# W block sums w21+w22 and (w21+w22)-w11 of the up projection: issued on POOL instead of DVE

## The chip, the core and the metric

One core of a Trainium2 chip runs the whole program. The metric is the device time of one execution in microseconds (us). Engines in the profile: PE is the matrix engine (PEld its weight loads), DVE the vector engine, ACT the scalar engine, POOL the GpSimd engine, SP the queue that issues most DMAs.

## The reference

A trunk of two layers works on 1024 tokens of width 1024. Each layer is an attention mixer followed by a squared-ReLU MLP, with norms, shifts, scales and gates around both. The change touches the first half of the MLP only:

```python
def squared_relu_mlp(h, w_up, w_down):      # w_up: 1024 x 4096, w_down: 4096 x 1024
    a = jax.nn.relu(h @ w_up)
    return (a * a) @ w_down
```

## The kernel before

**Seven products in place of eight.** `h @ w_up` is done for two hidden tiles of 128 at a time, called a pair, `q` = 0 to 15. Tokens (two halves of 512), input width (two halves of 512) and the two hidden tiles give a 2x2x2 block product, which is computed by Winograd's scheme with seven half-size products, named 1, 2, 6, 5, 7, 3, 4 in their order. They need four sums of weight blocks per pair. w11, w21 (first half of the width, first and second hidden tile) come with one DMA, w12, w22 with another. Sum 1 is w21+w22 (line 1322), sum 2 is sum 1 - w11 (line 1323), sum 3 is w11-w21 (line 1329), sum 4 is w12 - sum 2 (line 1333). Product 6 takes sum 2, product 5 sum 1, product 7 sum 3, product 3 sum 4. Each sum is a tile `ws` of 128x512 f32.

**Preparation of a product.** `prep(i)` (line 1306) forms the sum if the product needs one, then ACT rounds it to the high part (line 1339, tile `wt`), DVE subtracts that from the sum to get the low part (line 1340), and PE runs 12 matmuls for the product (`mm3`, lines 572 to 574: high x high, high x low, low x high, four times). The low part is the stationary operand of line 574. `before(i)` issues `prep` for a product `AHEAD` = 3 products ahead of its use, and the load of a pair some two products before that.

**What follows a product.** `evac` (line 1370 on DVE, from the matmul's bank; 1372, 1382 and 1383 on ACT) adds, applies ReLU and squares, into tiles `u`. After product 4 of a pair, `combine` forms five sums of the squared halves on POOL (line 1415 four times, tiles `sx`; line 1426 once, tile `sy`), which SP writes to DRAM (lines 1419 to 1427) for the down projection.

**Stretches.** Products 1 and 2 of the first six pairs (`PAIRS0`) run first, so a pair of the first six has only five products left when its sums are needed; the other ten pairs have seven. Beside them runs a side load (`ada`, lines 311 to 323): DMA loads `adaw` and DVE multiplies and adds.

**Order.** The order in the code is a list of steps that spreads preparations, products and side work; the framework then arranges the instructions of each engine by its own estimates of their times, so that POOL's order in the trace is not that of the code. At run time every engine and every queue takes its instructions in order. Tiles come from shared rings: 40 slots (`wt`, `u`, `sx`, the second half of the weights), 3 `raw` tiles (`adaw` and the first half of the weights), 8 `t2` tiles (`ws`, `sy`). A new tile waits for the last reader of the one that it replaces.

Of the kernel before, what the change touches and what calls it, by code (L numbers as in the profile page):

```python
# [93 lines left out]
class Trunk:  # L94
# [1126 lines left out]
    def up_setup(self, w_up, col):  # L1221
# [6 lines left out]
        nc = self.nc  # L1228
# [77 lines left out]
        def prep(i):  # L1306

            q, p = order[i]
            w = wraw[q]
            early = i < at[0]  # L1310
            t = nc.vector.tensor_tensor

            def new(n):
                sums[n] = four(self.t2("ws"))
                return sums[n]

            if p == 1:
                r = w[11]
            elif p == 2:
                r = w[12]  # L1320
            elif p == 6:
                t(new(1), w[21], w[22], op=ALU.add)
                t(new(2), sums[1], w[11], op=ALU.subtract)
                r = sums[2]
            elif p == 5:
                r = sums.pop(1)
            elif p == 7:
                r = new(3)
                nc.gpsimd.tensor_tensor(r, w.pop(11), w.pop(21), op=ALU.subtract)
                sums.pop(3)  # L1330
            elif p == 3:
                r = new(4)
                nc.gpsimd.tensor_tensor(r, w.pop(12), sums.pop(2), op=ALU.subtract)
                sums.pop(4)
            else:
                r = w.pop(22)
            s = self.slot("wt", F32R, [P, 2, 512])
            hi, lo = (four(s[:, y]) for y in range(2))
            nc.scalar.activation(hi, r, AF.Copy)  # L1339
            nc.vector.tensor_tensor(lo, r, hi.bitcast(F32), op=ALU.subtract)  # L1340
            left[i] = s
            if early and p == 2 or p == 4:
                wraw.pop(q)
# [5 lines left out]
        def before(i):  # L1349

            out = [lambda n=n: prep(n) for n in range(len(order)) if when(n) == i]
            if i in (0, 1, 2):
                out += [lambda q=q: load(q, True) for q in (3 + i,) if q < PAIRS0]
            for q in range(n_q):
                if i == (2 if q == 0 else when(at[q] - 2)):
                    out.append(lambda q=q: load(q, False))
            return out
# [479 lines left out]
```

## Time and profile before

| | us |
|---|---|
| median of three runs | 2547.33 |
| lowest, highest | 2542.2, 2547.57 |
| the profiled execution | 2548.21 |
| its span, first to last instruction | 2546.4 |
| PE busy | 2399.9 (94%) |
| DVE busy | 1924.9 (76%) |
| ACT busy | 1403.2 (55%) |
| POOL busy | 1325.5 (52%) |

The table's busy times are sums over the span. Matmuls are pipelined and their ends are modelled, so that the idle time in front of a PE instruction says more than PE's busy share. A wait names the instruction that released it.

### The profile page before, as it was taken

The numbers are of one execution on the slowest core, as the hardware profiler recorded it, in microseconds if no ns is written. First come the engines' busy times: TensorE is split into PE (matmuls) and PEld (weight loads), VectorE is DVE, ScalarE is ACT, GpSimd is POOL, SyncE is SP. The second block draws the span as 40 slices with busy tenths as digits, with TensorE's granted clock in tenths as the row PEclk, the third lists the DMA queues.
The fourth block names the chain that finished last, engine by engine and source line by source line (L and its number), as shares of the span: only waits on it lengthen the run. The fifth ranks groups of instructions, "written<-read, shape, count | busy, mean of one in ns | idle before, by whom it ended". The sixth has DMA issues, their size and how long they took to land.

```text
span 2546.4 us, 36695 instructions
## 1 busy us (share of the span) xinstructions
PE 2399.9 (94%) x11974; PEld 1991.6 (78%) x11974; DVE 1924.9 (76%) x3723; ACT 1403.2 (55%) x2959; POOL 1325.5 (52%) x1308
## 2 busy tenths in 40 slices
PE   6989999999998988999999999978999899999997
PEld 4779788888887766777778887867877688888886
DVE  7866479999895477877899768667767766787756
ACT  4632268888983463444435445367876355545433
POOL 4320566564672146555764722577744654594533
PEclk8999999999999999999999999998999999999999
DMA  7367723131226635556888754444323545597654
GB/s 279 100 224 229 237 88 96 39 92 42 84 71 149 141 116 189 201 191 201 321 324 324 236 189 163 138 128 125 75 76 128 186 168 183 192 318 240 230 183 173
DMA packets 239288, 437.15 MB, mean 172 GB/s; under 512 B 19236, under 2 KB 122872, under 8 KB 239096
## 3 DMA queue, kind: packets, MB, share of 16 engines
q1 hardware_dynamic: 210296, 405.44, 47.3%
q0 software_dynamic: 28800, 29.36, 4.8%
q8 instruction: 94, 1.54, 0.2%
q14 instruction: 98, 0.80, 0.1%
HBM read 320.42 MB, written 114.31 MB: 171 GB/s over the span
## 4 chain that ended last, share of the span: by engine, by line
PE 40%; DVE 6%; POOL 3%; issue 2%; DMA 2%; ACT 2%; SPq 0%; POOLq 0%; DVEq 0%; ACTq 0%
PE b L574 13%; PE b L572 13%; PE b L573 12%; POOL sx L1415 1%; DVE ada L323 1%; PE b L880 1%; DMA w<-in_mlp_w_up_dram 1%; DVE hl L1251 1%; PE o L925 1%; DVE p L884 1%; PE b L903 1%; DVE wt L1340 1%; DMA adaw<-in_ada_w_dram 0%; POOL qv L637 0%; POOL wr L1473 0%
## 5 line engine op out<-in xcount | busy, mean ns | idle before, releaser
L572 PE MATMUL b<-hh,wt 128*128 128x512 f32 x896 | 355.0, 396 | 17.0 <-ACT wt L1339 16.9
L574 PE MATMUL b<-hh,wt 128*128 128x512 f32 x896 | 350.9, 395 | 11.9 <-DVE wt L1340 11.6
L573 PE MATMUL b<-st,st 128*128 128x512 f32 x896 | 350.3, 391 | 4.9 <-DVE st L1489 4.9
L573 PE MATMUL b<-hl,wt 128*128 128x512 f32 x896 | 352.1, 393 | 0.0
L574 PE MATMUL b<-st,st 128*128 128x512 f32 x896 | 349.0, 390 | 0.0
L572 PE MATMUL b<-st,st 128*128 128x512 f32 x896 | 330.7, 390 | 1.6 <-DVE u L1370 1.6
L888 ACT ACTIVATE p<-p,nm 128x256 f32<-128x256 f32 (+7 forms) x384 | 250.7, 657 | 56.5 <-DVE nm L884 55.3
L1028 POOL TENSOR_SCALAR p<-p,rl,nsam 128x640 f32<-128x640 f32 (+7 forms) x256 | 199.5, 791 | 139.5 <-DVE rl L1026 93.1
L910 DVE TENSOR_TENSOR pT<-b,pT 128x512 fp32r<-128x512 f32 (+1 forms) x334 | 215.0, 657 | 19.5 <-ACT pT L909 19.1
L1488 ACT ACTIVATE st<-wr 128x1024 fp32r<-128x1024 f32 (+1 forms) x128 | 122.6, 958 | 193.2 <-POOL wr L1474 87.4
L1489 DVE TENSOR_TENSOR st<-wr,st 128x1024 fp32r<-128x1024 f32 (+1 forms) x128 | 188.3, 1471 | 53.6 <-ACT st L1488 30.1
L1489 DVE TENSOR_TENSOR st<-sr,st 128x1024 fp32r<-128x1024 f32 (+1 forms) x128 | 200.4, 1566 | 33.0 <-ACT st L1488 30.8
L572 PEld LDWEIGHTS b<-hh,wt 128*128 128x128 f32 x896 | 170.1, 190 | 59.3 <-ACT wt L1339 25.4
L574 PEld LDWEIGHTS b<-hh,wt 128*128 128x128 f32 x896 | 169.9, 190 | 55.7 <-DVE wt L1340 20.5
L909 ACT ACTIVATE pT<-b 128x512 fp32r<-128x512 f32 (+1 forms) x334 | 186.3, 579 | 43.2 <-PE b L903 41.8
L573 PEld LDWEIGHTS b<-st,st 128*128 128x128 f32 x896 | 168.5, 188 | 42.4 <-DVE st L1489 7.8
L903 PE MATMUL b<-ident,p 128*128 128x128 f32 x1296 | 193.5, 273 | 5.7 <-DVE nm L884 4.1
L1340 DVE TENSOR_TENSOR wt<-ws,wt 128x512 fp32r<-128x512 f32 x128 | 139.5, 1101 | 77.4 <-ACT wt L1339 76.8
L572 PEld LDWEIGHTS b<-st,st 128*128 128x128 f32 x896 | 168.6, 188 | 37.2 <-DVE u L1370 2.4
L573 PEld LDWEIGHTS b<-hl,wt 128*128 128x128 f32 x896 | 170.1, 190 | 34.6
L574 PEld LDWEIGHTS b<-st,st 128*128 128x128 f32 x896 | 168.6, 188 | 34.9
L925 PE MATMUL o<-pT,kv 128*128 128x512 f32 x484 | 193.1, 437 | 1.8 <-DVE pT L910 1.4
(277 smaller groups left out, 6060.3 us busy)
## 6 DMA issues: line engine op xcount, KB each, us to landing
adaw<-in_ada_w_dram SPq DMA_DIRECT2D x96, 512.0 KB, 4.9
sr<-s SPq DMA_DIRECT2D x96, 512.0 KB, 4.7
wr<-in_mlp_w_down_dram SPq DMA_DIRECT2D x96, 512.0 KB, 5.9
w<-in_mlp_w_up_dram SPq DMA_DIRECT2D x76, 512.0 KB, 4.8
s<-sx SPq DMA_DIRECT2D x64, 512.0 KB, 4.0
x<-x SPq DMA_DIRECT2D x48, 512.0 KB, 3.8
s<-u SPq DMA_DIRECT2D x64, 256.0 KB, 2.3
we<-in_mlp_w_down_dram SPq DMA_DIRECT2D x64, 256.0 KB, 3.9
```

The lines of the kernel that those rows point to most:

```text
L572: mm(out, s[0], m[0], start=first, stop=False)
L573: mm(out, s[0], m[1], start=False, stop=False)
L574: mm(out, s[1], m[0], start=False, stop=last)
L888: self.nc.scalar.activation(p, p, AF.Exp, scale=-1.0, bias=nm, accum_out=l)
L903: nc.tensor.transpose(pt[:, g * P:(g + 1) * P], p[:, cols], self.ident)
L909: nc.scalar.activation(x[:, 0, 0:w], pt[:, 0:w], AF.Copy)
L910: nc.vector.tensor_tensor(x[:, 1, 0:w], pt[:, 0:w], x[:, 0, 0:w].bitcast(F32), op=ALU.subtract)
L925: nc.tensor.matmul(out, s, m[:, z], start=n == 0 and z == 0, stop=n == len(tiles) - 1 and z == 1)
L1028: nc.gpsimd.tensor_scalar(ps[g], ps[g], rl[:, g:g + 1], gate[:, g, b:b + 1], op0=ALU.mult, op1=ALU.mult)
L1340: nc.vector.tensor_tensor(lo, r, hi.bitcast(F32), op=ALU.subtract)
L1488: nc.scalar.activation(hi, r, AF.Copy)
L1489: nc.vector.tensor_tensor(lo, r, hi.bitcast(F32), op=ALU.subtract)
```

## The change

The function that `prep` calls for sums 1 and 2 becomes POOL's. Sums 3 and 4 are already on POOL, the low parts (line 1340) stay on DVE. Nothing else is edited.

```diff
             early = i < at[0]
-            t = nc.vector.tensor_tensor
+            t = nc.gpsimd.tensor_tensor
...
                 t(new(1), w[21], w[22], op=ALU.add)
                 t(new(2), sums[1], w[11], op=ALU.subtract)
```

Only the two calls of lines 1322 and 1323 use `t`.

## Rows read from the trace of the kernel before

**Rows 1.** The page's busy times of all engines over the span.
```profile
PE 2399.9 (94%) x11974; PEld 1991.6 (78%) x11974; DVE 1924.9 (76%) x3723; ACT 1403.2 (55%) x2959; POOL 1325.5 (52%) x1308
```
**Rows 2.** Busy time by stretch; columns: stretch, length, then busy us (instructions) of each engine.
```profile
925.00:1045.00 120.00, 107.40 (x458) 84.14 (x457) 97.07 (x111) 59.06 (x97) 63.19 (x39) 1.00 0.51 170
1045.00:1225.00 180.00, 175.26 (x780) 142.31 (x779) 134.99 (x177) 85.79 (x146) 94.76 (x64) 0.99 0.57 196
1925.00:2045.00 120.00, 108.95 (x451) 84.89 (x450) 90.70 (x105) 54.52 (x90) 61.52 (x42) 0.97 0.42 145
2045.00:2225.00 180.00, 180.00 (x802) 148.69 (x801) 124.37 (x164) 93.02 (x152) 97.42 (x70) 1.00 0.52 182
```
**Rows 3.** PE's waits, 925:1045, then 1925:2045: total us, times, longest us.
```profile
PE b L574 <- DVE wt L1340: 6.9, 6, 2.9
PE b L572 <- ACT wt L1339: 5.6, 4, 2.5
...
PE b L572 <- ACT wt L1339: 9.0, 7, 2.6
PE b L574 <- DVE wt L1340: 1.9, 3, 0.9
```
**Rows 4.** PE's wait for a high part in 1045:1225, same view.
```profile
PE b L572 <- ACT wt L1339: 0.3, 1, 0.3
```
**Rows 5.** Instructions by line, whole span: count, then ns min/median/max.
```profile
L1322 DVE TENSOR_TENSOR ws<-w,w x32: 673/692/1785, 929.9 to 2196.7; 128x512 f32<-128x512 f32 x32
...
L1329 POOL TENSOR_TENSOR ws<-w x32: 1295/1314/2312, 923.1 to 2211.4; 128x512 f32<-128x512 f32 x32
...
L1415 POOL TENSOR_TENSOR sx<-u,u x64: 1282/1734/2264, 962.4 to 2241.0; 128x512 f32<-128x512 f32 x64
```
**Rows 6.** DVE's groups in 925:1045: busy us, mean ns, idle before, releaser.
```profile
L1322 DVE TENSOR_TENSOR ws<-w,w 128x512 f32<-128x512 f32 x7 | 5.9, 841 | 9.0 <-DMA w<-in_mlp_w_up_dram 9.0
L1323 DVE TENSOR_TENSOR ws<-ws,w 128x512 f32<-128x512 f32 x7 | 5.3, 755 | 0.0
```
**Rows 7.** POOL's waits in 925:1045: total us, times, longest us.
```profile
POOL ws L1333 <- DVE ws L1323: 37.2, 6, 12.5
```
**Rows 8.** Timeline of one pass, by engine: start, us, instruction, [idle before, releaser].
```profile
972.62 0.69 DVE L1322 TENSOR_TENSOR ws<-w,w 128x512 f32<-128x512 f32 x1 [2.48 <-DMA w<-in_mlp_w_up_dram]
...
973.83 0.68 DVE L1323 TENSOR_TENSOR ws<-ws,w 128x512 f32<-128x512 f32 x1
...
974.65 1.27 POOL L1333 TENSOR_TENSOR ws<-w,ws 128x512 f32<-128x512 f32 x1 [5.48 <-DVE ws L1323]
...
975.29 0.50 PE L572 MATMUL b<-hh,wt 128*128 128x512 f32 x1 [2.49 <-ACT wt L1339]
```
**Rows 9.** Timeline of a pass of the second layer, DVE and PE.
```profile
2003.75 0.69 DVE L1322 TENSOR_TENSOR ws<-w,w 128x512 f32<-128x512 f32 x1 [1.88 <-DMA w<-in_mlp_w_up_dram]
...
2005.89 0.50 PE L572 MATMUL b<-hh,wt 128*128 128x512 f32 x1 [2.60 <-ACT wt L1339]
```
**Rows 10.** Timeline, DVE's longest wait for weights and PE's next wait.
```profile
952.55 0.69 DVE L1322 TENSOR_TENSOR ws<-w,w 128x512 f32<-128x512 f32 x1 [5.14 <-DMA w<-in_mlp_w_up_dram]
...
955.93 0.50 PE L574 MATMUL b<-hh,wt 128*128 128x512 f32 x1 [0.91 <-DVE wt L1340]
```
**Rows 11.** Two lines of DVE, whole span: ns min/median/max.
```profile
L1370 DVE TENSOR_TENSOR u<-b,u x224: 645/679/693, 923.6 to 2230.0; 128x512 f32<-128x512 f32 x112
...
L1340 DVE TENSOR_TENSOR wt<-ws,wt x128: 672/1106/1779, 943.1 to 2214.7; 128x512 fp32r<-128x512 f32 x128
```
**Rows 12.** Timeline of a later pass, DVE and POOL.
```profile
1074.80 0.69 DVE L1322 TENSOR_TENSOR ws<-w,w 128x512 f32<-128x512 f32 x1 [0.20 <-DMA w<-in_mlp_w_up_dram]
...
1081.22 1.29 POOL L1415 TENSOR_TENSOR sx<-u,u 128x512 f32<-128x512 f32 x1 [8.38 <-ACT u L1383]
```
**Rows 13.** Timeline of SP's queue, two neighbouring issues.
```profile
981.05 0.32 SPq L1421 DMA_DIRECT2D s<-sx  x1
982.74 0.38 SPq L547 DMA_DIRECT2D w<-in_mlp_w_up_dram  x1
```

## The prediction

> **What bounds the kernel now.** I read the page's busy times first: PE is busy for 94% of the span and no other engine for more than 76% [rows 1]. So a change on DVE or POOL counts only where PE stands still. Next come the stretches in which the up projection runs, two per layer [rows 2]. The first of each layer (925 to 1045 us and 1925 to 2045 us, the six pairs with five products left) leaves PE idle for 12.6 and 11.1 us of 120; the second leaves 4.7 us of 180 and nothing. A matmul takes 180/802 = 0.224 us in the stretch without a gap, so a product of 12 takes 2.7 us. The reader should see that all that this change can win or lose at small scale lies in some 24 us of idle time at the start of the two up projections, and that the other pairs, 18 or so of the 32 passes, stand behind a full PE.
>
> Then I read what ends PE's waits there [rows 3]. PE waits 14.6 us for high parts from ACT and 8.8 us for low parts from DVE. The largest are waits for the high part of product 6, and the timeline shows the chain that ends in one: the weights land, DVE forms sum 1 at 972.62, does one evacuation in between, forms sum 2 from 973.83 to 974.51, ACT rounds it, and PE starts at 975.29 after 2.49 us of idling [rows 8]. In the second layer the same chain starts at 2003.75 and ends in an idle time of 2.60 us [rows 9]. Seven of PE's waits for high parts follow a sum 2 in this way, four in the first layer and three in the second. In these passes POOL is idle too: it waits for sum 2 with sum 4 next in its queue, 5.48 us in the pass shown [rows 8] and 37.2 us in six passes of the first layer [rows 7]. After sum 4 come the five sums of `combine`, and SP's next load of weights stands behind the write of such a sum [rows 13]. So the early passes form a loop: load, sums 1 and 2, sum 4, five `combine` sums, next load. What makes sum 2 later makes the whole loop later, and PE with it.
>
> **The change, part by part.** It removes 64 sums from DVE, 32 per line, and adds 64 to POOL. No DMA, no semaphore value by hand and no tile is added.
>
> *Cost of a sum.* On DVE the median is 0.692 us, and the same shape on POOL takes 1.314 us at the median, 1.295 at the least and 2.312 at the most [rows 5].
>
> *The path in the early passes.* DVE's pair takes 0.841 + 0.755 = 1.60 us there by means [rows 6], and mostly an evacuation of 0.68 us stands between the two [rows 8, 11], which costs some 0.6 us: 2.2 us from the first start to the second end. POOL's pair has nothing in between: 2 x 1.314 = 2.6 us undisturbed. The lower bound of the change of path is thus +0.4 us, and with two evacuations in between, as at some passes, -0.2. The upper bound is a pair in which both POOL instructions are disturbed as the median `combine` sum is, 2 x 1.734 = 3.5 us [rows 5], so +1.3. I take +0.6 us, nearer the undisturbed end, since DVE has evacuations to do at that moment, which read a bank and show no disturbance (645 to 693 ns over 224 of them [rows 11]). Seven passes: 7 x 0.6 = **+4.2 us**, between -1.4 and +9.1.
>
> *What leaves DVE.* In the early passes DVE stands still for 9.0 us before sum 1, waiting for weights [rows 6], with evacuations and low parts queued behind it. That wait moves to POOL, where sum 4 and the `combine` sums are queued behind it; but POOL waits at this place today, for sum 2 [rows 7], so it costs nothing new. For DVE it is a gain where PE waited for a low part that stood behind it: at 952.55 DVE has waited 5.14 us and PE stands for 0.91 us at 955.93 [rows 10]. At the start of each layer's up projection DVE also does two sums less; I count 0.6 us for each layer, half of the 1.2 us that the two take from a full queue, because their POOL versions collide with the splits that DVE does there. Together **-2.1 us**, between 0 and -8.8 (all of PE's waits for low parts there [rows 3]).
>
> *The later passes.* Weights land at 1074.80 in the pass shown and POOL is idle until 1081.22, for 8.38 us [rows 12]. The two sums fit in that gap with 2.6 to 3.5 us, so POOL's own later work is not delayed. Sum 2 moves by about 1 us, against a lead of three products, 8.1 us. PE waits for a high part 0.3 us in all in 1045 to 1225 [rows 4]. So I cost some 18 passes at nothing; the cover is the gap on POOL, and what it costs without it is the third rival below.
>
> *Collisions.* The low part of a sum takes 1.106 us at the median, and 0.672 at the least [rows 11]; the `combine` sum takes 1.282 at the least and 1.734 at the median [rows 5]. Both have two inputs in SBUF and run beside each other, and a line whose input is a bank (1370) never varies [rows 11]. The Trainium skill, page "SBUF — State Buffer", section "Who interferes with whom", says that a DVE instruction with two SBUF inputs and a GpSimd instruction that reads SBUF exclude each other, and that the later one fully blocks until the first is done. By that rule a POOL sum that meets a low part would take 1.314 + 0.68 = 2.0 us, a pair 4.0 us, and the sum for seven passes would be +12.5 us where the row's 1.734 gives +9.1. The trace agrees on who collides, and has a smaller price for one collision. In the sum above I have counted a quarter of these collisions.
>
> *The sum.* +4.2 - 2.1 = +2.1 us against the profiled execution's 2548.21 (its span of 2546.4 and 1.8 around it): 2550.3. That execution lies 0.9 above the median of 2547.33, so the median after the change is put at **2549.4**, with bounds of -1.4 - 8.8 = -10.2 and +9.1 from the two parts, 2537 to 2556. The low end is the first rival's; the forecast's own range begins at 2542.
>
> **The rivals.**
>
> *DVE's queue was the limit (faster).* If PE's waits for low parts, 8.8 us [rows 3], vanish because DVE no longer stands behind the weights, and the sums start the moment that the weights land, the path is not longer at all: 2547.3 - 8.8 = 2538.5. For it: DVE is busy for 97 of 120 us in 925 to 1045 and POOL for 63 [rows 2]. Against it: of DVE's 9.0 us before sum 1, 5.1 lie in the one pass already counted [rows 10], and 2.5 in a pass that ends in PE's wait for the high part [rows 8], which a longer pair doesn't shorten.
>
> *Collisions on both sides (slower).* If POOL's sums run beside low parts in all early passes, a pair takes 3.5 us: 7 x 1.3 = 9.1 us, and each of two low parts per pass takes 0.43 us more (1.106 - 0.672) on a path that PE waits for: 7 x 0.86 = 6.0. Together +15: 2562. It decides from the point at which DVE has low parts and not evacuations to do while the sums run. For it: half of the low parts from sums are already that slow [rows 11]. Against it: line 1370 stands between the two sums today.
>
> *POOL's order (slower).* The arrangement could put sums 1 and 2 behind `combine` sums in the later passes. Three to five of them are 5.2 to 8.7 us by the median [rows 5]. The lead of 8.1 us has 2.6 for the sums, 0.8 for the high part (974.51 to 975.29 [rows 8]) and 1.1 for the low part [rows 11] in it, which leaves 3.6; PE would stand for 1.6 us or more in each of some 18 passes, +29: 2576 and above. It decides once a third `combine` sum stands ahead of sum 1. For it: POOL's order is not that of the code. Against it: the weights land some 6 us before the first `combine` sum can start [rows 12].
>
> That the change doesn't do what it says is not to be feared: `t` has two uses, both seen on DVE [rows 6].
>
> **How the numbers follow.** The forecast, a longer pair in some seven passes and a small relief of DVE, has a chance of 0.50; its own range is 2542 to 2556. The first rival has 0.24, the collisions 0.18, POOL's order 0.08. The smallest change that a measurement of this kernel can tell from none is about 0.2%, 5.1 us, so "same" means 2542.2 to 2552.4. The forecast lies in it with 0.42 and above it with 0.08. Hence faster 0.24, same 0.42, slower 0.08 + 0.18 + 0.08 = 0.34. The range reaches to both nearer rivals and leaves the third out: 2538 to 2563.
>
> **What would show it.** Right: lines 1322 and 1323 on POOL at 1.3 to 1.8 us each, in the early passes directly ahead of sum 4, whose wait for sum 2 is gone and a wait for weights in its place; PE's waits for high parts up by 2 to 8 us in the early stretches, those for low parts down by about 2, and the later stretches as full as before. Wrong: PE idle in 1045 to 1225 or 2045 to 2225 with sum 2 behind `combine` sums; or waits for low parts gone altogether and the first stretches shorter by 5 us or more; or a difference that lies outside the up projections, since the arrangement of the instructions may change elsewhere too.

## The result, and the profile after

| | before | after |
|---|---|---|
| median of the timed runs beside each other (us) | 2546.05 | 2559.76 |
| profiled execution, span (us) | 2548.21, 2546.4 | 2559.81, 2558.0 |

The change makes the kernel slower: ratio 1.0051, 95% interval [1.0039, 1.0064], that is 13.7 us by the medians and 11.6 us between the two profiled spans. The forecast was 2549.4, with a range of its own from 2542 to 2556; the time lies outside that, and inside the wide range (2538 to 2563) only in the part that was added for the slower rivals.

The busy times of the page of after answer to [rows 1]:

```profile
PE 2405.8 (94%) x11974; PEld 1999.6 (78%) x11974; DVE 1927.8 (75%) x3659; ACT 1406.1 (55%) x2959; POOL 1425.2 (56%) x1372
```

DVE lost 64 instructions and no busy time, while POOL gained 100 us. Both up projections by stretch (columns as in [rows 2]; the second layer is taken 10 us later, since it starts later):

```profile
925.00:1045.00 120.00, 102.77 (x414) 80.63 (x413) 86.81 (x89) 54.10 (x89) 80.02 (x51) 0.94 0.49 160
1045.00:1225.00 180.00, 176.69 (x777) 144.09 (x777) 135.50 (x156) 86.35 (x145) 122.78 (x82) 0.98 0.57 197
1935.00:2055.00 120.00, 107.60 (x447) 85.26 (x446) 85.52 (x90) 53.82 (x89) 82.08 (x55) 0.94 0.42 143
2055.00:2235.00 180.00, 180.00 (x802) 148.74 (x801) 126.84 (x145) 93.65 (x153) 125.49 (x89) 1.00 0.52 181
```

The reader should look at the first row's number of matmuls, 414 where [rows 2] has 458, and at its granted clock, 0.94 where [rows 2] has 1.00. PE's waits in the first, second, third and fourth of these stretches (total us, times, longest) answer to [rows 3, 4]; the fourth has none:

```profile
PE b L574 <- DVE wt L1340: 9.2, 3, 4.4
PE b L572 <- ACT wt L1339: 7.9, 4, 3.4
...
PE b L574 <- DVE wt L1340: 3.0, 2, 2.7
...
PE b L572 <- ACT wt L1339: 0.3, 1, 0.3
...
PE b L572 <- ACT wt L1339: 11.8, 4, 5.6
...
PE b L574 <- DVE wt L1340: 0.6, 1, 0.6
```

**Where the time went.** I put the n-th up-projection matmul of one trace beside the n-th of the other. A layer has 1344; "early" is the 420 (35 products) from the 127th to the 547th, "late" the 794 from there to the 1341st. PE's timeline then splits a stretch in three: steps with an idle time in front (waits), steps of about 0.43 us with none (PE at the lower of its two clock levels, 1.2 GHz; at 2.4 GHz a step is 0.227 us), and the rest. Worked out so from one trace each, in us:

| | length before | after | waits | lower clock |
|---|---|---|---|---|
| first layer, early | 111.9 | 121.8 (+9.9) | 14.1 in 10 → 18.2 in 7 | 0 → 5.9 (28 matmuls) |
| first layer, late | 189.1 | 188.5 (-0.6) | 5.3 → 3.8 | 1.4 → 2.6 |
| second layer, early | 113.3 | 113.5 (+0.2) | 12.6 in 10 → 12.5 in 4 | 2.8 → 4.1 |
| second layer, late | 180.5 | 180.5 (0) | 0 → 0 | 0 → 0 |

So 9.9 of the 11.6 us lie in the early passes of the first layer, and there in two parts: 4.1 us of longer waits, and 5.9 us lost because PE works at half its clock behind some of them. The other 2.1 us are spread outside these four stretches. The timeline of after shows both parts at once; here is the pass that answers to [rows 8], start, us, instruction, and in brackets the idle time before it with its releaser:

```profile
974.51 1.26 POOL L1322 TENSOR_TENSOR ws<-w,w 128x512 f32<-128x512 f32 x1 [4.98 <-DMA w<-in_mlp_w_up_dram]
975.86 1.26 POOL L1323 TENSOR_TENSOR ws<-ws,w 128x512 f32<-128x512 f32 x1
...
977.81 2.79 DVE L1340 TENSOR_TENSOR wt<-ws,wt 128x512 fp32r<-128x512 f32 x2 [5.42 <-ACT wt L1339]
977.83 0.59 PE L572 MATMUL b<-hh,wt 128*128 128x512 f32 x1 [3.42 <-ACT wt L1339]
978.23 0.63 PE L573 MATMUL b<-hl,wt 128*128 128x512 f32 x1
...
978.65 0.63 PE L572 MATMUL b<-hh,wt 128*128 128x512 f32 x1
```

From the first sum's start to PE it is 977.83 - 974.51 = 3.32 us, where [rows 8] gives 975.29 - 972.62 = 2.67: the path grew by 0.65 us, as forecast. What was not forecast is on the other lines. DVE no longer stands in front of the sums, waiting for weights; it stands 5.42 us in front of a low part, waiting for ACT and through it for POOL, with everything that comes after it in its queue. And PE's matmuls behind the wait follow each other in 0.42 us.

The second kind of place is a pass later. DVE's side work (line 323) ran ahead of two low parts in the kernel before, at 992.32; the framework's estimates now put it behind them, and they wait for POOL's sum 2. It runs at 997.86, and the next one, behind two more low parts, at 1003.50 (997.14 in the kernel before). That one frees the raw tile for the side load issued at 1005.83 (998.44 in the kernel before), which is what DVE waits for next:

```profile
997.86 2.31 DVE L323 SCALAR_TENSOR_TENSOR ada<-adaw,cond,ada 128x1024 f32<-128x1024 f32 x1
...
1005.83 0.33 SPq L311 DMA_DIRECT2D adaw<-in_ada_w_dram  x1
...
1010.82 1.28 DVE L323 SCALAR_TENSOR_TENSOR ada<-adaw,cond,ada 128x1024 f32<-128x1024 f32 x1 [3.14 <-DMA adaw<-in_ada_w_dram]
1012.02 0.68 DVE L1340 TENSOR_TENSOR wt<-w,wt 128x512 fp32r<-128x512 f32 x1
...
1012.75 0.79 PE L574 MATMUL b<-hh,wt 128*128 128x512 f32 x1 [4.36 <-DVE wt L1340]
1013.35 0.63 PE L572 MATMUL b<-hh,wt 128*128 128x512 f32 x1
1013.77 0.63 PE L573 MATMUL b<-hl,wt 128*128 128x512 f32 x1
```

The low part at 1012.02 belongs to a block that needs no sum at all. PE waits 4.36 us for it, and a second wait of the same kind, 3.96 us, ends at 1032.20. The waits in front of the half-clock runs of the first layer's early passes are 1.83, 3.42, 4.36 and 3.96 us; behind the other three of the seven (0.86, 1.79, 0.91) the clock did not fall, and behind none of the ten of the kernel before, the longest 2.92 us.

### The profile page after: what moved, and what is told of

Its sections match the earlier page's. It is cut to its first block, busy times and chain, and to the rows that moved or that the text cites. A ratio compares the mean times of both kernels' runs of the same rounds, so it can differ in the third digit from the quotient of the medians.

```text
span 2558.0 us, 36730 instructions
## 1 busy us (share of the span) xinstructions
PE 2405.8 (94%) x11974; PEld 1999.6 (78%) x11974; DVE 1927.8 (75%) x3659; ACT 1406.1 (55%) x2959; POOL 1425.2 (56%) x1372
## 4 chain that ended last, share of the span: by engine, by line
PE 39%; DVE 5%; POOL 4%; issue 3%; DMA 3%; ACT 1%; SPq 0%; POOLq 0%; DVEq 0%; ACTq 0%
PE b L572 12%; PE b L573 12%; PE b L574 12%; DMA w<-in_mlp_w_up_dram 1%; POOL sx L1415 1%; DMA wr<-in_mlp_w_down_dram 1%; PE b L880 1%; DVE p L884 1%; PE b L903 1%; DVE ada L323 1%; PE o L925 0%; POOL qv L637 0%; DVE wt L1340 0%; DMA adaw<-in_ada_w_dram 0%; DVE hl L1251 0%
## 5 line engine op out<-in xcount | busy, mean ns | idle before, releaser
L1489 DVE TENSOR_TENSOR st<-sr,st 128x1024 fp32r<-128x1024 f32 (+1 forms) x128 | 205.6, 1606 | 32.4 <-ACT st L1488 30.2
L910 DVE TENSOR_TENSOR pT<-b,pT 128x512 fp32r<-128x512 f32 (+1 forms) x334 | 215.0, 657 | 17.9 <-ACT pT L909 17.5
```

The costliest lines, as they stand in the source:

```text
L910: nc.vector.tensor_tensor(x[:, 1, 0:w], pt[:, 0:w], x[:, 0, 0:w].bitcast(F32), op=ALU.subtract)
```

## The experiments

The ratio of each is to the kernel before, run on the same chip beside it. Lengths of stretches are worked out as above, from one trace each.

**Which passes carry it.** Sums 1 and 2 on POOL for the first six pairs only, and for the other ten only.

```diff
-            t = nc.vector.tensor_tensor
+            t = (nc.gpsimd if q < PAIRS0 else nc.vector).tensor_tensor    # e1; e2: q >= PAIRS0
```

> Sums 1 and 2 on POOL for the first six pairs only, on DVE for the other ten. Theory (the early loop): the whole loss of some 13 us lies in the early passes, where POOL's queue sets when the next weights and low parts come; so this kernel is as slow as the change, ratio about 1.005. Rival (collisions everywhere, or a rearrangement of the later passes): the loss goes with the number of sums moved, 12 of 32, so a ratio of about 1.002.

> Sums 1 and 2 on POOL for the last ten pairs only (20 of 32 passes). Theory (the early loop): within 0.1% of the kernel before, because PE is full in the later stretches and POOL has a gap there. Rival (collisions or rearrangement): 20 of 32 of the loss, ratio about 1.003.

Measured: the early pairs alone 2553.65 us, ratio 1.0030 [1.0019, 1.0042]; the later pairs alone 2547.47, ratio 1.0008 [0.9999, 1.0017]. In the first, the first layer's early passes are 122.9 us long (+11.0), with 17.9 us of waits and 39 matmuls at half clock, 7.9 us; in the second they are 112.1 with none. So most of the loss that can be placed is the early pairs', and the ten later pairs cost nothing that can be told from nothing, as the prediction had it. By the run times the early pairs have 0.0030 of the 0.0051, between what theory and rival asked for; both parts add up to 0.0038, and whether the rest is more than noise the intervals don't tell.

**Is it the place of sum 3?** POOL's order changed: before, sum 3 ran while POOL waited for sum 2; in after it stands between sum 2 and sum 4. One kernel issues it ahead of sums 1 and 2, the other gives it to DVE.

```diff
             elif p == 6:
+                nc.gpsimd.tensor_tensor(new(3), w[11], w[21], op=ALU.subtract)    # e3
...
-                nc.gpsimd.tensor_tensor(r, w.pop(11), w.pop(21), op=ALU.subtract)
+                r = sums.pop(3)    # e3, in place of this call
+                nc.vector.tensor_tensor(r, w.pop(11), w.pop(21), op=ALU.subtract)    # e4
```

> The change, but sum 3 (w11-w21, which needs only the first half of the weights) is issued ahead of sums 1 and 2, so that POOL does it while it waits for the second half. Theory A (place of sum 3): after the change sum 3 stands between sum 2 and sum 4 and puts 1.3 to 1.7 us more into each early pass; taken out, five or six passes of the first layer give back some 7 us, ratio about 1.002. Theory B (the pair itself is longer, and collisions): no gain, ratio 1.005.

> The change with sum 3 on DVE in exchange: POOL has one sum more than before instead of two. Theory A (what counts is how many sums POOL does between the weights and combine): as with sum 3 ahead, ratio about 1.002. Theory B (pair length and collisions): the pair on POOL stays, so 1.004 to 1.005. Rival C (POOL's total work): half of the loss goes, 1.0025.

Measured: 2564.89, ratio 1.0077 [1.0060, 1.0093], and 2581.16, ratio 1.0142 [1.0126, 1.0157]; both are slower than any theory had them. The first is no clean test, since the framework put sum 3 amid the `combine` sums and not ahead of sum 1; its first early passes are 120.1 us. With sum 3 on DVE they are 115.8, still 3.8 above before, but 28 us are lost in the two late stretches (+11.5, +16.4), where nothing had been lost. Its DVE then waits for the side's loads in 2060 to 2250:

```profile
DVE ada L323 <- DMA adaw<-in_ada_w_dram: 17.3, 5, 3.6
ACT wt L1339 <- DMA w<-in_mlp_w_up_dram: 15.5, 6, 5.1
```

Neither run makes the loss go: sum 3 earlier in POOL's queue brings 1.7 us of 9.9, and on DVE 6.0, which can have three reasons (POOL has a sum less per pass, the raw tile whose last reader sum 3 is comes free sooner, the order is another), and is lost again where the side loads and DVE's queue meet. The place of sum 3 alone is not shown to be a cause; the side loads are what both traces name, and the next runs take them.

**Are the side loads part of it?** The first layer's up projection has 24 of them beside it, the second layer's 8. They are begun 20 products later, on the kernel before and on the change.

```diff
-            (ramp if i < 2 * PAIRS0 + 10 else steps).extend(own)
+            (ramp if i < 2 * PAIRS0 + 30 else steps).extend(own)
```

> The kernel before, with the side loads (adaw and their sums on DVE) starting after the early passes instead of two pairs into them. Reference for the next run. Both theories: the first layer's early passes get no longer than the 112 us that they take before (PE's matmuls 126 to 546 of the up projection), perhaps some us shorter; the whole may be a little slower or faster since the side work is denser later, within 0.4%.

> The change, with the side loads starting after the early passes. Theory S (the loss comes from the side loads in the early passes of the first layer, which wait for a raw tile that POOL now frees and hold up DVE's queue): the early passes take within 2 us of those of the run before with the sums on DVE, and the kernel is within 0.15% of it. Rival L (the loop over POOL alone, longer pair and sum 3 in it): the early passes stay 8 to 10 us longer than with the sums on DVE, and the whole 0.35 to 0.5% slower than it.

Measured: on the kernel before 2535.09, ratio 0.9961 [0.9947, 0.9976], faster than both kernels; on the change 2550.12, ratio 1.0018 [1.0008, 1.0027]. The change costs 15.0 us here by the medians, as much as before: the loss moves and does not go. The difference that the sums make, POOL less DVE:

| | first early | first late | second early | second late |
|---|---|---|---|---|
| side loads as they were | +9.9 | -0.6 | +0.2 | 0 |
| side loads late | +4.2 | +10.4 | +1.5 | +4.0 |

The early loss falls from 9.9 to 4.2 us (2.3 of it waits, 1.6 lower clock), and a new one appears in the late passes, to which the side loads have moved. So much of it follows the side loads; 4.2 is more than theory S allows and less than rival L asks for, so the early passes have a part that does not. In the late passes of the change (1045 to 1247) and of the kernel with the sums on DVE (1041 to 1233), in this order:

```profile
PE b L574 <- DVE wt L1340: 7.8, 8, 2.4
PE b L572 <- ACT wt L1339: 4.9, 4, 2.0
...
PE b L574 <- DVE wt L1340: 4.7, 4, 2.7
...
PE b L572 <- ACT wt L1339: 0.5, 1, 0.5
```

**Through which resource?** Two couple the side loads to the sums: the three raw tiles, of which the weights' is now freed by POOL's sum 3, and DVE's queue. Two pairs were made. The first gives the ring a fourth raw tile, and one slot less to the others for lack of room:

```diff
-SLOTS = 40
+SLOTS = 39
...
-    nraw = 3
+    nraw = 4
```

> The kernel before with four raw tiles instead of three and 39 slots instead of 40. Reference for the next run. Expected within 0.5% of the kernel before; if the raw ring is what the early passes wait for, some us faster in the first layer's early passes.

> The change with four raw tiles and 39 slots. Theory R (the raw ring carries the loss: POOL frees the first half of the weights later, so the next load and the next adaw start later): the early passes of the first layer are within 4 us of those with four raw tiles and the sums on DVE. Rival L (POOL's own chain between the weights and combine): they stay 8 to 10 us longer.

Measured: 2571.78 with the sums on DVE, ratio 1.0114 [1.0091, 1.0136], and 2588.02 on POOL, 1.0172 [1.0157, 1.0187]. POOL costs only 0.9 us in the first early passes, which is in theory R's range, but 11.3 in the second layer's late ones. These early passes take 119.3 us with the sums on DVE already, 7.4 more than in the kernel before, and the two edits together cost either kernel some 27 us, twice what the change did and more than the 0.5% expected. Another limit may hide POOL's here: inconclusive. The second pair leaves both counts alone, and takes the tiles of the side loads from the slots:

```diff
-                u[k] = (raw or self.raw)("adaw")
+                u[k] = self.slot(name="adaw") if single else (raw or self.raw)("adaw")
```

> The kernel before, but the tiles adaw of the side loads come from the 40 slots instead of the three raw tiles, so a side load waits for no weight sum any more, and a load of weights for no side load. The slots carry up to three tiles more. It is the base for the run that does the same with sums 1 and 2 on POOL; the difference of the two is what counts. By itself: the first layer's early passes 111.9 us in the kernel before; with the raw ring as one of the limits there, 104 to 111; with the slots as the tighter ring, 112 to 118. In all 2540 to 2556.

> The change, with the tiles adaw of the side loads from the slots. Ring theory: the change's loss of 9.9 us in the first layer's early passes comes mostly because POOL's sum 3 now frees the raw tile that the next side load waits for; then here the difference to the same kernel with the sums on DVE falls to 3 to 5 us there, as without the side loads (4.2), and DVE's waits for adaw are no longer than in that kernel. Queue theory: the loss comes because the side's multiply-adds and the low parts share DVE's queue, and one of them waits for POOL's sums with the other behind it; then the difference stays at 7 to 11 us there. In either case the second layer's early passes differ by less than 2 us.

Measured: 2559.59, ratio 1.0064 [1.0048, 1.0079], and 2567.68, ratio 1.0098 [1.0081, 1.0115]. The first is slower than the 2540 to 2556 that were expected; both lose some 24 us in the first late passes, where PE waits three times for the end of a side load (line 349, for `adas`: 24.4 and 24.2 us). Why it comes so late there was not followed up, so only the difference of the two counts: +7.5 us in the first early passes, +1.4 in the second's, some 1 us in each late stretch. 7.5 is in the range of the queue theory and outside that of the ring. Split as above, it is 2.6 us of waits (12.8 → 15.4) and 4.8 of lower clock (0 → 24 matmuls). By this pair the ring has some 1.5 us of the waits (4.1 less 2.6, from one trace each), and the rest stays without it. The pair with four raw tiles doesn't bear this out, nor can it speak against it. DVE's stand is the plainest difference; 925 to 1045, DVE's wait for a high part, with the sums on DVE and then on POOL:

```profile
DVE wt L1340 <- ACT wt L1339: 4.3, 5, 1.9
...
DVE wt L1340 <- ACT wt L1339: 23.0, 10, 5.4
```

The same wait in the kernel before, and in after:

```profile
DVE wt L1340 <- ACT wt L1339: 4.5, 5, 1.9
...
DVE wt L1340 <- ACT wt L1339: 17.3, 8, 5.4
```

**Does PE's standing lower the clock?** On the change, PE is given work to do in the waits ahead of product 6: twelve matmuls on old data, whose result the product overwrites.

```diff
                 hi, lo = R[p][j]
+                for _ in range(12 * (j == 0 and p == 6 and q < PAIRS0)):
+                    nc.tensor.matmul(banks[i], hi[:, 0, 0:P], hi[:, 0], start=True, stop=True)
```

> The change, with twelve extra matmuls of 128x512 in front of each product 6 of the first six pairs of each layer, on data that are long there; the product's own first matmul overwrites what they leave in the bank. They are extra work, 12 x 0.227 = 2.7 us in each of twelve places, and they run in the time in which PE otherwise waits for sum 2 (in the first layer of the changed kernel 1.83, 3.42 and 1.79 us). It tells what lowers the granted clock there. If PE's standing still does, the matmuls 0.43 us apart that follow the waits ahead of product 6 (15 of 28 in the first layer's early passes) go: 0 to 13 are left, and the granted clock of 937 to 975 us is 1.00. If something else does (the load on memory, POOL's work), 24 or more are left. In time the fillers are a loss either way: those six of the first layer take 16.3 us, some 6.3 of it in waits, so that its early passes take 125 to 129 us in the first case and 130 to 133 in the second; the whole 2567 to 2582.

Measured: 2572.05, ratio 1.0096 [1.0080, 1.0113]. In the first early passes 8 matmuls run at half clock, 1.6 us, where after has 28 and 5.9; in the second's 7, where after has 18. The granted clock of 937 to 955, 955 to 975, 975 to 995, 995 to 1015 and 1015 to 1035 us is 0.91, 1.00, 0.91, 0.93 and 0.93 in after; with the fillers (the clock stands third from the right):

```profile
937.00:955.00 18.00, 18.00 (x81) 14.89 (x80) 13.39 (x18) 11.41 (x19) 0.09 (x1) 1.00 0.28 88
955.00:975.00 20.00, 19.07 (x85) 15.46 (x84) 8.93 (x13) 6.88 (x12) 12.28 (x9) 1.00 0.34 117
975.00:995.00 20.00, 19.75 (x86) 15.69 (x85) 12.98 (x14) 6.67 (x12) 16.23 (x11) 1.00 0.51 173
995.00:1015.00 20.00, 16.51 (x71) 12.80 (x70) 14.62 (x16) 7.35 (x13) 11.80 (x8) 1.00 0.70 221
1015.00:1035.00 20.00, 15.85 (x61) 12.04 (x60) 11.46 (x10) 5.24 (x9) 14.09 (x9) 0.91 0.49 162
```

The first early passes take 125.5 us, the forecast of the first case: 72 x 0.227 = 16.3 us of extra matmuls lengthen them by 3.8, the others are paid by waits (18.2 → 10.5) and by the clock. So it is PE's standing still that lowers the clock here. The length of a wait alone doesn't tell: one of 3.31 us that ends at 1011.27, with fillers soon behind it, is not followed by a slower matmul, and one of 1.89 us that ends at 1018.90 is followed by seven. As a remedy the fillers fail: the second layer's early passes grow by 7.0 us, and the whole is slower than the change.

**A faster version.** Away from POOL: the kernel before with the side loads late, and sum 4 of the first six pairs on DVE.

```diff
-                nc.gpsimd.tensor_tensor(r, w.pop(12), sums.pop(2), op=ALU.subtract)
+                (nc.vector if q < PAIRS0 else nc.gpsimd).tensor_tensor(r, w.pop(12), sums.pop(2), op=ALU.subtract)
...
-            (ramp if i < 2 * PAIRS0 + 10 else steps).extend(own)
+            (ramp if i < 2 * PAIRS0 + 30 else steps).extend(own)
```

> The kernel before with the side loads begun 20 products later, and sum 4 of the first six pairs on DVE, right behind sum 2: the change's idea turned round. What hangs on it: in the kernel before, POOL waits 37.2 us in the first layer's early passes for sum 2, with the five combine sums behind sum 4. If the loop of sums, combine and next load limits these passes, taking sum 4 out of POOL's queue shortens them by a further 2 to 6 us in both layers together, 2529 to 2534 against 2535.1 of the kernel with the side loads late. If DVE's queue limits them, six sums of 0.69 us per layer come on top, 2536 to 2544. If neither, 2533 to 2537.

Measured: 2530.61, ratio 0.9952 [0.9937, 0.9967], in the range of the first case. It beats both kernels; whether it beats the one with the side loads late alone (0.9961 [0.9947, 0.9976]) can't be told. Its two early stretches are 103.0 and 102.7 us, with 6.9 and 3.6 us of waits.

## Why the prediction was off

**The path.** Right, in size too. Over the seven pairs of sums that start in 925 to 1045 us the time from the start of sum 1 to the end of sum 2 is 2.47 us on average before and 2.98 after: +0.51 a pass, where +0.6 was forecast, and 7 x 0.51 = 3.6 against +4.2. The sums take 1.37 and 1.62 us at the median over the whole span:

```profile
L1322 POOL TENSOR_TENSOR ws<-w,w x32: 1262/1369/2297, 926.3 to 2208.5; 128x512 f32<-128x512 f32 x32
```

PE's waits for high parts rose by 2.3 us in the first layer and 2.8 in the second [rows 3], inside the 2 to 8 us forecast. One reading was off: the longest single wait of the kernel before, 2.92 us at 995.47, is for a low part, not for the high part of product 6. The sums are not "directly ahead of sum 4": sum 3 stands between, and what that costs alone the runs don't settle.

**DVE's relief.** This step failed: -2.1 us were forecast, and in the first layer PE's waits for low parts rose from 6.9 us [rows 3] to 9.2; only the second's fell, from 1.9 to 0.6. The working followed DVE's 9.0 us of waiting for weights [rows 6] to POOL and took them for gone on DVE. They came back as a wait for what POOL makes of the weights, 17.3 us in place of 4.5, one step further down the same chain. The prediction named the queue behind the wait that moves to POOL, but not the queue behind the low parts that stay on DVE and now wait for POOL: evacuations, the low parts of blocks without a sum, and the side work. The runs with the side loads late show that the side work makes this dearer; the pair with their tiles elsewhere puts some 1.5 us of it down to the tile ring, from one trace each.

**Collisions.** Counted at a quarter, and by a reading that the trace doesn't bear out. Put beside POOL's instructions, the low parts fall into two groups, in both kernels. One that meets no POOL instruction takes 0.64 to 0.69 us. One that starts while POOL is inside a sum (at least 0.05 us after its start and 0.12 before its end) ends 0.55 us after the end of that sum (0.54 to 0.56), in all 93 cases before and all 132 after. An evacuation, one of whose two inputs is a bank, is not held: all 224 take 0.645 to 0.695 us in either kernel. In after, a sum of POOL that ends at 1031.60, a low part that it holds until 1032.15, and PE's wait of 3.96 us that ends with it:

```profile
1029.36 2.24 POOL L1329 TENSOR_TENSOR ws<-w 128x512 f32<-128x512 f32 x1
...
1030.40 1.75 DVE L1340 TENSOR_TENSOR wt<-w,wt 128x512 fp32r<-128x512 f32 x1
...
1032.20 0.50 PE L574 MATMUL b<-hh,wt 128*128 128x512 f32 x1 [3.96 <-DVE wt L1340]
```

So the rule of the Trainium skill that the prediction weighed (page "SBUF — State Buffer", section "Who interferes with whom": the port pair that the two engines share is an exclusive lock) is what the trace shows, and "a smaller price for one collision" was misread: the later instruction waits for what is left of the earlier one, so that the 0.68 + 1.31 = 1.99 us of the rule, an estimate, is the worst case and a median of 1.106 means that most meet partway or not at all. This ate DVE's gain. In 1045 to 1225 sums 1 and 2 were 7.1 + 7.1 = 14.2 us of DVE's time; the low parts of blocks without a sum, before and after:

```profile
L1340 DVE TENSOR_TENSOR wt<-w,wt 128x512 fp32r<-128x512 f32 x27 | 17.5, 675 | 0.0
...
L1340 DVE TENSOR_TENSOR wt<-w,wt 128x512 fp32r<-128x512 f32 x28 | 31.4, 1154 | 0.3 <-ACT wt L1339 0.3
```

31.4 - 17.5 = 13.9 us, about as much as left. Where the loss lies it changed less: in the first layer's early passes the low parts are held, beyond 0.68 us each, for 13.6 us in all before and 16.6 after. Of that, 1.1 us is in the wait of 3.96 us just shown (1.75 - 0.68).

**The clock.** The term that the sum lacked. [rows 2] shows a granted clock of 1.00 in the first layer's early passes and 0.97 in the second's; the prediction priced PE's waits by their length, and nothing else. In after they are fewer and longer, seven for 18.2 us in place of ten for 14.1, and 28 matmuls behind them run at 1.2 GHz, 0.43 in place of 0.227 us: 5.9 us, more than the 4.1 by which the waits themselves grew. The fillers show that it is the standing that does it; which waits the clock falls behind, the runs don't settle. The Trainium skill describes this loss (page "TensorE: Matmul & The Clock Gate", section "HAM oscillation — how this bites in real kernels": waits for data between bursts of matmuls send TensorE back to its low clock, and each burst starts slow again); this trace agrees in four of the seven waits, behind which a matmul takes 0.42 to 0.43 us.

**The later passes.** Right: PE waits for high parts 0.3 us in 1045 to 1225 as before [rows 4], the last stretch is full, and the later pairs alone cost nothing that could be told (1.0008 [0.9999, 1.0017]). That the gap on POOL [rows 12] covers the sums there fits this, and POOL's order, the third rival, didn't turn against them.

**The rivals.** None is what happened. Collisions on both sides came nearest by time (2562), but their mechanism asks for pairs of 3.5 us, and the pair is 2.98. That the time lies inside the wide range is therefore luck: its upper end was drawn for them. Put together afterwards, which is a check of the terms and no test: the forecast's own path, the relief at nothing, and 5.9 + 1.3 us for the clock in the two early stretches give 2549.4 + 2.1 + 7.2 = 2558.7, against 2559.76.

**What stays open.** The 2.1 us outside the four stretches are from one trace each, and the first matmul of the up projection comes 4.1 us later in one trace (899.3) than in another (895.3), of kernels that have the same instructions up to there. That the order of DVE's queue by itself costs the 2.6 us of waits was argued from the timeline; no run fixes that order by hand. The shares of queue and ring rest on one pair of runs that is itself disturbed later on.

## What to carry to other kernels

When an instruction moves to another engine, look at what stays behind and consumes its result: it now waits in its own in-order queue for the other engine, and everything behind it waits too, related or not. Price a wait of PE not by its length alone: read the granted clock of the stretch, and add the matmuls that run at half clock behind the wait. And where instructions that stay read two inputs from SBUF beside the moved ones, don't count the moved work as time that the first engine gets back.

## What the hardware showed that I had not expected

The low parts on DVE and the sums on POOL take turns: in 225 of 225 cases a low part that started inside a POOL sum ended 0.55 us after it. So DVE's busy time did not fall when 64 sums, 49.3 us, left it (1924.9 to 1927.8 us): the low parts of blocks without a sum alone grew from 74.2 to 106.0 us over the span, and the time for which low parts are held, beyond 0.68 us each, from 65 to 100 us.

A few longer waits were worse for PE in the first layer than many short ones of nearly the same sum: ten for 14.1 us left the clock at 1.00, seven for 18.2 us lowered it, which cost 5.9 us on top. It is no rule by number: in the second layer ten waits for 12.6 us lost 2.8 us to the clock, and four for 12.5 us lost 4.1. Extra matmuls in such waits can be cheap, 16.3 us of them for 3.8 in the first layer's early passes, but the same number cost 7.0 us in the second's.
